# RWKV-7 time mixing: whole 128-row triangular inverses formed ahead of the chains, in place of four multiplications inside each chain

## The chip, the cores and the metric

The kernel runs on one core of a Trainium2 chip. The metric is the device time of one execution in microseconds; the median of three runs stands for the kernel. The core has five engines with queues of their own: TensorE (PE in the profile, its weight loads PEld), VectorE (DVE), ScalarE (ACT), GpSimd (POOL) and SyncE (SP). Each engine takes its instructions in the order of its queue. Matrix products are written to PSUM, a small memory of eight banks, and copied out by ACT or DVE.

## The reference

One decoder layer on 256 tokens of width 2048, all in float32: a SwiGLU feed-forward block, a mixer, a cross-attention into 256 memory rows, a second SwiGLU block, and a final norm. The mixer adds a sliding-window attention and an RWKV-7 time mixing (16 heads of size 64), both gated. What matters here is the recurrence of the time mixing:

```python
def step(S, inp):
    r_t, w_t, k_t, v_t, a_t, b_t = inp
    sa = jnp.einsum('bhij,bhj->bhi', S, a_t)
    S = S * w_t[:, :, None, :] + sa[..., None] * b_t[:, :, None, :] + v_t[..., None] * k_t[:, :, None, :]
    return S, jnp.einsum('bhij,bhj->bhi', S, r_t)
```

Within a block of 128 tokens, the vectors `sa` of all tokens depend on each other through a strictly lower triangular matrix L of 128 x 128 for each head (the products of every `a_t` with every earlier `b_s`, decays included). They solve (I - L) sa = u, where u is known from the values and from the state at the block's start. So each head and block needs the inverse of a triangular 128 x 128 matrix, or its product with u.

## The kernel before, in words

Every large product (feed-forward, projections) splits weights and activations into a high and a low part and multiplies high by high, low by high and high by low: the three lines L407, L408 and L409 in `times`. The weights stream in from memory through SP, ACT casts the high part (L319), DVE subtracts to get the low part (L320), and TensorE takes two of the weight tiles with their three products each at a time. After each six products `product` calls `bg.tick()`.

`Interleave` (`bg`) holds small pieces of other work as Python generators in named groups; a tick lets the first few generators of each group run to their next `yield`, group by group in the order of their declaration. So a `yield` puts about six weight products between two steps, and `idle(n)` puts n ticks there. This sets the order in which the program is written. A planner then orders each engine's queue by its own estimate of the times: what is written first goes first where it is ready, and work that is written later moves ahead where the engine would idle. The buffers are counted per tag (`t4` has 20 of 4 KB a partition); a new tile waits until one is free. The DVE steps of `substitute`, for example, run well before the weight products beside which they are written.

The 1024 features of the time mixing are two halves `h` of eight heads; one `pair(h, j)` treats two heads, e = 0 and 1, and walks through the two blocks c of 128 tokens. Steps that the change touches:

- `removal_keys` (group `ew`) forms L for each half and block and stores it in the DRAM tensor `ld`, rows t, columns s.
- `substitute` loads the 32 x 32 blocks on the diagonal of all 32 matrices, inverts them by 31 steps of forward substitution on DVE (L1125, L1130), and stores them transposed in `xd` (L1132): four blocks i, 32 matrices, u and t.
- `inverse_blocks(h, c)`, called by `pair(h, 0)` for both c, fills two tiles of eight heads on the POOL queue: `x`, the four inverted diagonal blocks (two memsets L1201 and L1202, loads L1205), and `r`, the parts of L to the left of them (loads L1207).
- `pair` masks the products of keys and receptances (`mk`, L1240, from the L177 products, written alternately from rows 0-63 and 64-127 into two banks), forms u (L1249, L1251) and, in the same bank, nt, the product of r and x (L1253): the part of L outside the diagonal blocks, multiplied by the inverted diagonal. It is nilpotent in four steps of 32 rows. So four `stage`s (L1266, each followed by the ACT copy L1271 and a `yield`) give sa: x times u, and then three times nt times the last result plus what was there. The last steps are y (L1290 to L1299) and, for c = 0, the state for the second block (L1283 to L1302).
- `finish` normalizes y for two pairs and multiplies by the gate.

At most three chains (`pair`) run at a time. `substitute`, `receptances` and `values` stand one behind another in the group `ew`; a chain starts when `values(h)` has ended. Beside the chains TensorE does the weight products of r, v and four gates (`L1366`).

Of the kernel before, what the change touches and what calls it, by code (L numbers as in the profile page):

```python
# [7 lines left out]
F32 = mybir.dt.float32  # L8
# [7 lines left out]
P = 128  # L16
# [123 lines left out]
def decoder_layer(ctx: ExitStack, tc: tile.TileContext, a: dict, out: bass.AP):  # L140
    nc = tc.nc
    act, dve, pool, pe = nc.scalar, nc.vector, nc.gpsimd, nc.tensor
# [6 lines left out]
    dram = ctx.enter_context(tc.tile_pool(name="dram", bufs=1, space=DRAM))  # L149
    bg = Interleave()  # L150
    bg.group("const", 1)
    bg.group("feat", 1)
    bg.group("attn", 2)
    bg.group("ew", 1)
    bg.group("chain", 3)
    bg.group("norm", 1)
    bg.group("mem", 1)
# [7 lines left out]
    def mm():  # L165
        return ps.tile([P, 512], F32, tag="mm", name="mm")

    def tr():
        return ps.tile([P, 512], F32, tag="tr", name="tr", bufs=2)
# [9 lines left out]
    def wait_for(name):  # L179
        while name not in bg.seen:  # L180
            yield

    def idle(n):
        for _ in range(n):
            yield
# [38 lines left out]
    for e in range(2):  # L224
        q = slice(64 * e, 64 * e + 64)
# [43 lines left out]
    for entry in weight_plan(a):  # L269
# [4 lines left out]
        w, k0, nk, c0, n = entry  # L274
# [489 lines left out]
    grd = dram.tile([T, D], F32, name="grd")  # L764
    ld = dram.tile([P, 32, P], F32, name="ld")
    xd = dram.tile([4, 32, 32, 32], F32, name="xd")

    def aligned(sp):

# [3 lines left out]
    with tc.tile_pool(name="f1", bufs=1, reuse_waits="tile") as sp:  # L773
        aligned(sp)
        at["pool"] = sp
        x = sp.tile([P, 2, D], F32, name="x")
# [4 lines left out]
        n1 = Norm(g_ffn1)  # L781
# [36 lines left out]
        n2 = hold["n"]  # L818
# [4 lines left out]
    with tc.tile_pool(name="mx", bufs=1, reuse_waits="tile") as sp:  # L823
        aligned(sp)

        def t4(name, shape=(P, 4, T), dt=F32):
            return sp.tile(list(shape), dt, tag="t4", name=name, bufs=N4)
# [285 lines left out]
        def substitute():  # L1113
            yield from idle(4)
            dl = t4("dl", (P, 32, 32))
            for i in range(4):
                q = slice(32 * i, 32 * i + 32)
                pool.dma_start(dl[q], ld[q, :, q].rearrange("t h s -> h t s"))
            xt = t4("xt", (P, 32, 32))
            pool.memset(xt[:], 0.0)  # L1120
            pool.memset(xt[:].rearrange("p u t -> p (u t)")[:, 0 : 32 * 32 : 33], 1.0)
            yield from idle(14)
            tmp = t4("tmp", (P, 32, 32))
            for t in range(1, 32):
                dve.tensor_tensor(  # L1125
                    tmp[:, :t, :t], xt[:, :t, :t],
                    dl[:, t, :t].unsqueeze(1).to_broadcast([P, t, t]), ALU.mult,
                )
                yield
                dve.tensor_reduce(xt[:, :t, t], tmp[:, :t, :t], AX.X, ALU.add)  # L1130
                yield from idle(1 + t // 20)
            pool.dma_start(xd[:].rearrange("i h u t -> (i h) u t"), xt[:])  # L1132
            yield from idle(2)
            bg.seen.add("inverse")

# [59 lines left out]

        xb = {}

        def inverse_blocks(h, c):
            x, r = t4("xb", (P, 8, P)), t4("rb", (P, 8, P))
            o = slice(h * 16 + c * 8, h * 16 + c * 8 + 8)  # L1200
            pool.memset(x[:], 0.0)  # L1201
            pool.memset(r[:], 0.0)  # L1202
            for i in range(4):
                q = slice(32 * i, 32 * i + 32)
                pool.dma_start(x[q, :, q], xd[i, o].rearrange("h u t -> u h t"))  # L1205
                if i:
                    pool.dma_start(r[q, :, : 32 * i], ld[q, o, : 32 * i])  # L1207
            xb[h, c] = x, r

        def small(name):  # L1210
            return sp.tile([P, P], F32, tag="sm", name=name, bufs=14)

        rows = [slice(64 * e, 64 * e + 64) for e in range(2)]
        ek = dict(skip_group_check=True)
        yq = {}

        def pair(h, j):
            yield from wait_for("inverse")
            yield from wait_for(f"ready{h}")
            if j % 2 == 0:  # L1220
                yq[h, j // 2] = sp.tile([P, 2, T], F32, tag="yq", name="yq", bufs=3)
            y = yq[h, j // 2]
            if j == 0:
                for c in range(2):
                    inverse_blocks(h, c)
            if j < 3:
                yield from idle(3 + j)
            ah, bh, kh, rh = at_[h], bt[h], aa[h], rt[h]
            s0 = None
            for c in range(2):  # L1230
                cs_ = slice(c * P, (c + 1) * P)
                mk = sp.tile([P, 2, 3, P], F32, tag="mk", name="mk", bufs=3)
                b = [tr() for _ in range(2)]
                by_turns(
                    (b[e][:, m * P : (m + 1) * P], x1[r, j, cs_], x2[r, j, cs_])
                    for m, (x1, x2) in enumerate(((kh, ah), (kh, rh), (bh, rh)))
                    for e, r in ((1, rows[1]), (0, rows[0]))
                )
                for e in range(2):
                    dve.tensor_tensor(  # L1240
                        mk[:, e].rearrange("p m t -> p (m t)"), b[e][:, : 3 * P],
                        mask3[:].rearrange("p m t -> p (m t)"), ALU.mult,
                    )
                yield
                vp = vtok[h][:, c, j * P : (j + 1) * P]
                x, rr = xb[h, c]
                b = tr()
                for e, r in enumerate(rows):
                    pe.matmul(b[:, r], mk[:, e, 0, :], vp[:, r], start=e == 0, stop=c == 0, **ek)  # L1249
                if c:  # L1250
                    pe.matmul(b[:, :P], ah[:, j, cs_], s0[:], start=False, stop=True, **ek)  # L1251
                for e in range(2):
                    pe.matmul(  # L1253
                        b[:, (2 + e) * P : (3 + e) * P], rr[:, 4 * e + j, :], x[:, 4 * e + j, :],
                        start=False, stop=True, **ek,
                    )
                u = small("u")
                act.copy(u[:], b[:, :P])
                nt = sp.tile([P, 2, P], F32, tag="nt", name="nt", bufs=3)
                act.copy(nt[:], b[:, 2 * P :].rearrange("p (e t) -> p e t", e=2))  # L1260
                yield
                vb = mm()

                def stage(lhs, rhs, o, first, name):
                    for e, r in enumerate(rows):
                        pe.matmul(  # L1266
                            vb[:, o : o + P][:, r], lhs(e), rhs[:, r],
                            start=first and e == 0, stop=True, **ek,
                        )
                    s = small(name)  # L1270
                    act.copy(s[:], vb[:, o : o + P])  # L1271
                    return s

                v0 = stage(lambda e: x[:, 4 * e + j, :], u, 0, True, "v0")
                yield
                v1 = stage(lambda e: nt[:, e, :], v0, 0, False, "v1")
                yield
                w = stage(lambda e: nt[:, e, :], v1, P, False, "w")
                yield
                sa = stage(lambda e: nt[:, e, :], w, 0, False, "sa")  # L1280
                if c == 0:
                    b = tr()
                    pe.transpose(b[:, :P], bh[:, j, cs_], ident[:])  # L1283
                    pe.transpose(b[:, P : 2 * P], kh[:, j, cs_], ident[:])
                    bk = sp.tile([P, 2, P], F32, tag="bk", name="bk", bufs=3)
                    act.copy(bk[:], b[:, : 2 * P].rearrange("p (x f) -> p x f", x=2))
                yield
                b = tr()
                if c:
                    pe.matmul(b[:, :P], s0[:], rh[:, j, cs_], start=True, stop=False, **ek)  # L1290
                for e, r in enumerate(rows):
                    pe.matmul(b[r, :P], vp[:, r], mk[:, e, 1, :], start=c == 0, stop=False, **ek)
                for e, r in enumerate(rows):
                    pe.matmul(b[r, :P], sa[:, r], mk[:, e, 2, :], start=False, stop=True, **ek)
                if c == 0:
                    bs = b[:, P : 2 * P]
                    pe.matmul(bs, bk[:, 0, :], sa[:], start=True, stop=False, **ek)
                    pe.matmul(bs, bk[:, 1, :], vp, start=False, stop=True, **ek)
                act.copy(y[:, j % 2, cs_], b[:, :P])  # L1299
                if c == 0:  # L1300
                    s0 = small("s0")
                    dve.scalar_tensor_tensor(  # L1302
                        s0[:], bs, dec[h][:, j : j + 1], bdup[:], ALU.mult, ALU.mult
                    )
                yield
            bg.seen.add(f"y{4 * h + j}")
# [161 lines left out]
        for h in (0, 2):  # L1468
            b = tr()
# [120 lines left out]
```

## Time and profile before

| | us |
|---|---|
| median of three runs | 2262.45 (2262.22 to 2262.84) |
| the profiled execution | 2258.33 |
| its span | 2256.6 |
| TensorE busy in it | 2240.6 |
| the chains: first L1266 record to last | 1092.5 to 1263.4 |
| store of the 32-row inverses (L1132) | 1008.7 |

The profiled execution lies 4.1 us under the median, so a sum is made against 2258.33 and then moved by that much. A group's line gives the source line, engine, operation, tiles as output<-inputs, shape, count, busy time, the mean duration of one in ns, and the idle time before them with what ended it. For TensorE the shape begins with rows*columns of the array that the record uses, and one float32 product stands as two records, each with its weight load. Records overlap in time; the chain of work (start, duration, what) gives each piece only the time by which it came later than the piece before.

### The profile page before, as it was taken

To read this page: it belongs to the slowest core of one execution; us is meant where nothing else is said; L and a number is where in the kernel's file an instruction comes from. 1 tells how busy PE (TensorE), PEld (TensorE's weight loads), DVE (VectorE), ACT (ScalarE), POOL (GpSimd) and SP (SyncE) were. 2 spreads that over 40 slices of the span, in tenths; PEclk is the share of its full clock that TensorE was granted. 3 is DMA by queue.
4 is the path that set the end of the run, shared out by engine and by line. 5 is a ranking of instruction groups with operands and counts; after the bars stand their busy time and mean duration, and the time that the engine had idled before them with its cause. 6 is when DMAs were issued, how large, how long until landed. Compare 5 with 4: busy or idle time off the path is not lost.

```text
span 2256.6 us, 28302 instructions
## 1 busy us (share of the span) xinstructions
PE 2240.6 (99%) x10588; PEld 1836.1 (81%) x10588; DVE 1740.8 (77%) x2120; ACT 1213.3 (54%) x1611; POOL 130.9 (6%) x184
## 2 busy tenths in 40 slices
PE   9999999999999999999999999999999999999998
PEld 7888888888888777888888888888888888888886
DVE  7988988888987577795444566547898888898887
ACT  6555555555555576444344446556555455555554
POOL 1000000000000002201220030001000000000002
PEclk9999999999999999999999999999999999999999
DMA  7666665565566445766332576547555665555664
GB/s 246 212 223 196 204 207 188 185 212 199 202 199 198 144 143 163 242 207 196 116 108 88 175 258 240 188 159 268 191 203 187 205 204 187 201 195 201 205 203 152
DMA packets 219434, 434.63 MB, mean 193 GB/s; under 512 B 13744, under 2 KB 15872, under 8 KB 219296
## 3 DMA queue, kind: packets, MB, share of 16 engines
q1 hardware_dynamic: 210768, 406.37, 54.0%
q0 software_dynamic: 7952, 25.65, 3.6%
q8 instruction: 83, 1.36, 0.2%
q10 hardware_dynamic: 576, 0.79, 0.1%
q14 instruction: 55, 0.45, 0.1%
HBM read 419.65 MB, written 13.11 MB: 192 GB/s over the span
## 4 chain that ended last, share of the span: by engine, by line
PE 95%; DVE 3%; issue 1%; ACT 1%; DMA 1%; SPq 0%; POOLq 0%; POOL 0%; ACTq 0%; DVEq 0%
PE acc L407 19%; PE acc L409 19%; PE acc L408 19%; PE mm L408 8%; PE mm L409 8%; PE mm L407 8%; PE tr L604 2%; PE tr L408 2%; PE tr L409 2%; PE tr L407 2%; PE mm L1266 1%; DVE lo L320 1%; PE tr L177 1%; PE mm L177 1%; ACT hi L319 0%
## 5 line engine op out<-in xcount | busy, mean ns | idle before, releaser
L319 ACT CAST hi<-raw 128x1024 fp32r<-128x1024 f32 (+1 forms) x770 | 763.7, 1001 | 790.4 <-PE acc L409 387.8
L320 DVE TENSOR_TENSOR lo<-raw,hi 128x1024 fp32r<-128x1024 f32 (+1 forms) x770 | 890.0, 1166 | 369.8 <-ACT hi L319 368.6
L407 PE MATMUL acc<-hi,xhi 128*128 128x512 f32 (+1 forms) x1196 | 475.5, 398 | 2.1 <-ACT hi L319 1.9
L408 PE MATMUL acc<-lo,xhi 128*128 128x512 f32 (+1 forms) x1196 | 465.5, 389 | 1.0 <-DVE lo L320 0.8
L409 PE MATMUL acc<-hi,xlo 128*128 128x512 f32 (+1 forms) x1196 | 465.8, 389 | 0.0
L407 PEld LDWEIGHTS acc<-hi,xhi 128*128 128x128 f32 x1196 | 224.6, 188 | 51.1 <-issue 4.5
L409 PEld LDWEIGHTS acc<-hi,xlo 128*128 128x128 f32 x1196 | 224.5, 188 | 47.9 <-issue 1.7
L408 PEld LDWEIGHTS acc<-lo,xhi 128*128 128x128 f32 x1196 | 224.9, 188 | 46.2 <-DVE lo L320 2.3
L344 ACT CAST thi<-raw 128x1024 fp32r<-128x1024 f32 x160 | 166.0, 1052 | 68.2 <-DVE raw L339 33.3
L345 DVE TENSOR_TENSOR tlo<-raw,thi 128x1024 fp32r<-128x1024 f32 x160 | 192.8, 1218 | 1.3 <-ACT thi L344 1.3
L408 PE MATMUL acc<-lo,hhi 128*128 128x512 f32 x404 | 158.0, 391 | 0.0
L409 PE MATMUL acc<-hi,hlo 128*128 128x512 f32 x404 | 157.9, 391 | 0.0
L407 PE MATMUL acc<-hi,hhi 128*128 128x512 f32 x404 | 157.3, 392 | 0.0
L407 PE MATMUL mm<-hi,xhi 128*128 128x512 f32 x380 | 149.1, 392 | 0.0
L408 PE MATMUL mm<-lo,xhi 128*128 128x512 f32 x380 | 148.1, 390 | 0.0
L409 PE MATMUL mm<-hi,xlo 128*128 128x512 f32 x380 | 148.1, 390 | 0.0
L339 DVE TENSOR_TENSOR raw<-raw 128x1024 f32<-128x1024 f32 x80 | 97.5, 1219 | 19.1 <-DMA raw<-in_ffn_w_up_dram 18.4
L408 PEld LDWEIGHTS acc<-lo,hhi 128*128 128x128 f32 x404 | 75.8, 188 | 17.4 <-DVE lo L320 2.3
L407 PEld LDWEIGHTS acc<-hi,hhi 128*128 128x128 f32 x404 | 75.9, 188 | 16.0 <-DVE x L562 0.9
L409 PEld LDWEIGHTS acc<-hi,hlo 128*128 128x128 f32 x404 | 75.8, 188 | 15.5
L408 PEld LDWEIGHTS mm<-lo,xhi 128*128 128x128 f32 x380 | 71.4, 188 | 15.3 <-DVE lo L320 0.3
L409 PEld LDWEIGHTS mm<-hi,xlo 128*128 128x128 f32 x380 | 71.3, 188 | 14.7
(374 smaller groups left out, 3403.8 us busy)
## 6 DMA issues: line engine op xcount, KB each, us to landing
raw<-in_ffn_w_gate_dram SPq DMA_DIRECT2D x167, 512.0 KB, 3.6
raw<-in_ffn_w_up_dram SPq DMA_DIRECT2D x160, 512.0 KB, 4.6
raw<-in_ffn_w_down_dram SPq DMA_DIRECT2D x152, 512.0 KB, 4.7
raw<-in_w_in_dram SPq DMA_DIRECT2D x136, 512.0 KB, 3.5
raw<-in_w_out_dram SPq DMA_DIRECT2D x32, 512.0 KB, 4.3
raw<-in_ffn_w_down_dram SPq DMA_DIRECT2D x12, 1024.0 KB, 5.0
raw<-in_ffn_w_up_dram SPq DMA_DIRECT2D x8, 1024.0 KB, 6.5
raw<-in_w_proj_attn_dram SPq DMA_DIRECT2D x16, 512.0 KB, 3.5
```

Of the source, the lines that this page charges most:

```text
L177: prev = pe.matmul(*args, start=True, stop=True)
L319: newest["act"] = act.copy(hi[:, s], raw[:, s])
L320: newest["dve"] = dve.tensor_tensor(lo[:, s], raw[:, s], f32(hi[:, s]), ALU.subtract)
L339: dve.tensor_tensor(ta[:], raw[:, 1:3], raw[:, 0:2], ALU.subtract)
L344: act.copy(hi[:, s], t[:])
L345: dve.tensor_tensor(lo[:, s], t[:], f32(hi[:, s]), ALU.subtract)
L407: pe.matmul(o, xh, hi, start=first, stop=False, **how)
L408: pe.matmul(o, xh, lo, start=False, stop=False, **how)
L409: pe.matmul(o, xl, hi, start=False, stop=last, **how)
L604: pe.transpose(b[:, o : o + P], tok[:, t, col : col + P], ident[:])
L1266: pe.matmul(vb[:, o : o + P][:, r], lhs(e), rhs[:, r], start=first and e == 0, stop=True, **ek,)
```

## The change

`substitute` also stores the 32-row inverses the other way round (rows t, columns u) for the first three diagonal blocks, in a new DRAM tensor `xe`: ACT writes the transposed order into the finished scratch tile `tmp`, POOL stores it.

`inverse_blocks` becomes the generator `invert(h, c)` in a group of its own (one at a time, declared ahead of `chain`). It runs from the end of `substitute`, no longer from the first chain. It loads the diagonal blocks x, the blocks r of L, and the blocks xu from `xe`, waits four ticks, and completes the inverse for eight heads in two doublings. First, from 32 to 64 rows: r times x for the blocks 1 and 3 (16 products of 32 x 32, one bank, copied to n1), then a tick later xu times n1 for the blocks 2 and 0 (16 products) and the same product the other way round (8 products), one bank, copied back into x and xu. Then from 64 to 128 rows: 8 products of 64 x 64 and a copy to n2, a tick, 8 products of 64 x 64 and a copy into x. Each head's x is then the whole inverse of its 128-row triangle.

A chain no longer forms nt (L1253, L1260). It waits for its inverse and does one stage in place of four: sa is x times u. There are four ticks for a block in place of seven. The bank `vb` holds one result. The tag `sm` has 10 buffers instead of 14, `nt` is gone, and `xu`, `n1`, `n2` are new.

```diff
+    bg.group("inverse", 1)
     bg.group("chain", 3)
...
+    xe = dram.tile([3, 32, 32, 32], F32, name="xe")
...
             pool.dma_start(xd[:].rearrange("i h u t -> (i h) u t"), xt[:])
+            act.copy(tmp[:96], xt[:96].rearrange("p u t -> p t u"))
+            pool.dma_start(xe[:].rearrange("i h t u -> (i h) t u"), tmp[:96])
             yield from idle(2)
             bg.seen.add("inverse")
...
-        def inverse_blocks(h, c):
-            x, r = t4("xb", (P, 8, P)), t4("rb", (P, 8, P))
+        def invert(h, c):
+            yield from wait_for("inverse")
+            x, r = t4("xb", (P, 8, P)), t4("rb", (P, 8, 96))
+            xu = sp.tile([P, 8, 64], F32, tag="xu", name="xu", bufs=2)
             o = slice(h * 16 + c * 8, h * 16 + c * 8 + 8)
+            q = [slice(32 * i, 32 * i + 32) for i in range(4)]
             pool.memset(x[:], 0.0)
-            pool.memset(r[:], 0.0)
-            for i in range(4):
-                q = slice(32 * i, 32 * i + 32)
-                pool.dma_start(x[q, :, q], xd[i, o].rearrange("h u t -> u h t"))
+            pool.memset(xu[q[0]], 0.0)
+            for i in (1, 3, 2, 0):
+                pool.dma_start(x[q[i], :, q[i]], xd[i, o].rearrange("h u t -> u h t"))
                 if i:
-                    pool.dma_start(r[q, :, : 32 * i], ld[q, o, : 32 * i])
-            xb[h, c] = x, r
+                    pool.dma_start(r[q[i], :, : 32 * i], ld[q[i], o, : 32 * i])
+            for i, to in ((0, q[0]), (2, q[0]), (1, q[1])):
+                pool.dma_start(xu[q[i], :, to], xe[i, o].rearrange("h t u -> t h u"))
+            yield from idle(4)
+
+            def several(bank, products):
+                for to, lhs, rhs in products:
+                    pe.matmul(bank[to], lhs, rhs, start=True, stop=True)
+
+            def cols(n, w):
+                return slice(n * w, n * w + w)
+
+            def heads(bank, rows, w):
+                return bank[rows, : 8 * w].rearrange("p (n t) -> p n t", n=8)
+
+            b = tr()
+            several(b, (
+                ((q[i - 1], cols(n, 32)), r[q[i], n, q[i - 1]], x[q[i], n, q[i]])
+                for n in range(8) for i in (1, 3)
+            ))
+            n1 = sp.tile([P, 8, 32], F32, tag="n1", name="n1", bufs=2)
+            act.copy(n1[q[0]], heads(b, q[0], 32))
+            act.copy(n1[q[2]], heads(b, q[2], 32))
+            yield
+            b = tr()
+            several(b, (
+                ((q[i], cols(n, 32)), xu[q[i], n, q[0]], n1[q[i], n, :])
+                for n in range(8) for i in (2, 0)
+            ))
+            several(b, (
+                ((q[1], cols(n, 32)), n1[q[0], n, :], xu[q[0], n, q[0]]) for n in range(8)
+            ))
+            act.copy(x[q[2], :, q[3]], heads(b, q[2], 32))
+            act.copy(x[q[0], :, q[1]], heads(b, q[0], 32))
+            dve.tensor_copy(xu[q[1], :, q[0]], heads(b, q[1], 32))
+            yield
+            low, high = slice(0, 64), slice(64, 128)
+            b = tr()
+            several(b, (
+                ((low, cols(n, 64)), r[high, n, low], x[high, n, high]) for n in range(8)
+            ))
+            n2_ = sp.tile([64, 8, 64], F32, tag="n2", name="n2", bufs=1)
+            act.copy(n2_[:], heads(b, low, 64))
+            yield
+            b = tr()
+            several(b, (((low, cols(n, 64)), xu[low, n, :], n2_[:, n, :]) for n in range(8)))
+            act.copy(x[low, :, high], heads(b, low, 64))
+            xb[h, c] = x
+            yield
+            bg.seen.add(f"inverse{h}{c}")
+
+        for h in range(2):
+            for c in range(2):
+                bg.spawn("inverse", invert(h, c))
...
         def pair(h, j):
-            yield from wait_for("inverse")
             yield from wait_for(f"ready{h}")
...
             if j == 0:
-                for c in range(2):
-                    inverse_blocks(h, c)
-            if j < 3:
-                yield from idle(3 + j)
+                yield from wait_for(f"inverse{h}0")
+            elif j < 3:
+                yield from idle(j)
...
-                for e in range(2):
-                    pe.matmul(
-                        b[:, (2 + e) * P : (3 + e) * P], rr[:, 4 * e + j, :], x[:, 4 * e + j, :],
-                        start=False, stop=True, **ek,
-                    )
                 u = small("u")
                 act.copy(u[:], b[:, :P])
-                nt = sp.tile([P, 2, P], F32, tag="nt", name="nt", bufs=3)
-                act.copy(nt[:], b[:, 2 * P :].rearrange("p (e t) -> p e t", e=2))
                 yield
...
-                v0 = stage(lambda e: x[:, 4 * e + j, :], u, 0, True, "v0")
-                yield
-                v1 = stage(lambda e: nt[:, e, :], v0, 0, False, "v1")
-                yield
-                w = stage(lambda e: nt[:, e, :], v1, P, False, "w")
-                yield
-                sa = stage(lambda e: nt[:, e, :], w, 0, False, "sa")
+                yield from wait_for(f"inverse{h}{c}")
+                x, vb = xb[h, c], mm()
+                for e, r in enumerate(rows):
+                    pe.matmul(
+                        vb[:, r], x[:, 4 * e + j, :], u[:, r], start=e == 0, stop=True, **ek
+                    )
+                sa = small("sa")
+                act.copy(sa[:], vb[:, :P])
```

More of the change, by code (lines that the diff above doesn't have):

```diff
@@ L1210, in small @@
+            act.copy(x[low, :, high], heads(b, low, 64))
[5 more added lines that the diff above has]
+                bg.spawn("inverse", invert(h, c))
         def small(name):
-            return sp.tile([P, P], F32, tag="sm", name=name, bufs=14)
+            return sp.tile([P, P], F32, tag="sm", name=name, bufs=10)
         rows = [slice(64 * e, 64 * e + 64) for e in range(2)]
@@ L1245, in pair @@
                 vp = vtok[h][:, c, j * P : (j + 1) * P]
-                x, rr = xb[h, c]
                 b = tr()
@@ L1251, in pair @@
                     pe.matmul(b[:, :P], ah[:, j, cs_], s0[:], start=False, stop=True, **ek)
-                for e in range(2):
-                    pe.matmul(
-                        b[:, (2 + e) * P : (3 + e) * P], rr[:, 4 * e + j, :], x[:, 4 * e + j, :],
-                        start=False, stop=True, **ek,
-                    )
                 u = small("u")
                 act.copy(u[:], b[:, :P])
-                nt = sp.tile([P, 2, P], F32, tag="nt", name="nt", bufs=3)
-                act.copy(nt[:], b[:, 2 * P :].rearrange("p (e t) -> p e t", e=2))
                 yield
[L1262 to L1272, printed above, removed]
-                v0 = stage(lambda e: x[:, 4 * e + j, :], u, 0, True, "v0")
-                yield
-                v1 = stage(lambda e: nt[:, e, :], v0, 0, False, "v1")
-                yield
-                w = stage(lambda e: nt[:, e, :], v1, P, False, "w")
-                yield
-                sa = stage(lambda e: nt[:, e, :], w, 0, False, "sa")
+                yield from wait_for(f"inverse{h}{c}")
[6 more added lines that the diff above has]
+                act.copy(sa[:], vb[:, :P])
                 if c == 0:
```

## The prediction

> **What bounds the kernel now.** I read the page first, then the waits of TensorE in the stage that the change touches, then the chain of work of that stage.
>
> ```profile
> span 2256.6 us, 28302 instructions
> PE 2240.6 (99%) x10588; PEld 1836.1 (81%) x10588; DVE 1740.8 (77%) x2120; ACT 1213.3 (54%) x1611; POOL 130.9 (6%) x184
> PEclk9999999999999999999999999999999999999999
> PE 95%; DVE 3%; issue 1%; ACT 1%; DMA 1%; SPq 0%; POOLq 0%; POOL 0%; ACTq 0%; DVEq 0%
> ```
>
> TensorE is busy 99% of the span at full clock and carries 95% of the chain that ended last. The recurrence runs in 1086 to 1273 us, so I take 1050 to 1290 (240 us) as its stage. These are TensorE's waits there (engine, line, waited for, total, times, longest), and busy times in one stretch (PE, PEld, DVE, ACT, POOL):
>
> ```profile
> PE tr L1249 <- DVE mk L1240: 0.2, 1, 0.2
> 1080.00:1120.00 40.00, 40.00 (x270) 32.13 (x270) 18.62 (x29) 15.56 (x36) 4.63 (x9) 1.00 0.34 103
> ```
>
> One wait of 0.2 us in 240: although a chain waits four times in a row for its own copies, TensorE always has a weight product or another chain's step to run meanwhile. DVE, ACT and POOL are under half busy. So shortening a chain's latency is worth nothing by itself; the change is worth the TensorE time that it takes out, less what it puts in. Busy time counts overlapping instructions twice, so I price by the chain of work, whose pieces do not overlap. Its shares of the 240 us:
>
> ```profile
> by line: PE acc L407 20.0%; PE acc L409 18.9%; PE acc L408 18.3%; PE mm L1266 11.6%; PE tr L177 7.2%; PE tr L1253 3.2%; PE tr L1336 2.9%; PE tr L1249 2.8%; PE tr L1292 2.5%; PE tr L1178 1.5%; PE tr L1294 1.5%; PE tr L1327 1.4%; PE tr L1186
> ```
>
> **Removed from TensorE.** Records of the two lines (two records per fp32 matmul: L1253 issues 16 x 2 matmuls and has 64):
>
> ```profile
> L1266 PE MATMUL mm<-v,nt 128*128 128x64 f32 x128 | 17.6, 267 | 0.0
> L1253 PE MATMUL tr<-xb,rb 128*128 128x128 f32 x64 | 10.2, 282 | 0.0
> L1266 PE MATMUL mm<-u,xb 128*128 128x64 f32 x64 | 9.7, 273 | 0.0
> L1266 PE MATMUL mm<-w,nt 128*128 128x64 f32 x64 | 9.3, 268 | 0.0
> ```
>
> L1253 goes whole: 3.2% of 240 = 7.7 us. Of L1266's 256 records only the 64 of the first stage (u) stay: three quarters of 11.6% of 240 = 20.9 us. A third, small term comes from how the pieces stand:
>
> ```profile
> 1086.39 0.87 PE tr L177 x12
> 1087.26 0.43 PE acc L407
> 1087.68 0.23 PE acc L408
> ...
> 1089.73 0.41 PE tr L177 x2
> 1090.14 0.43 PE acc L407
> ...
> 1092.59 0.59 PE mm L1266 x4
> 1093.18 0.29 PE acc L407
> 1093.46 0.23 PE acc L408
> ...
> 1107.24 0.22 PE tr L1294 x4
> ```
>
> A weight product after a full-width stage costs 0.29 instead of 0.23 us. Some 15 such places go, as an estimate from 48 stages that mostly stand in groups: 0.9 us. Removed together: 29.5 us.
>
> **Added to TensorE.** Each of the four inverses (two half layers, two token blocks) issues, for its 8 heads: 16 products of 32x32, then 16 + 8 of 32x32, then 8 and 8 of 64x64. That is 80 narrow and 32 half-wide records, 320 and 128 in all. No such shape is in the trace; the ladder of shapes that are there:
>
> - full width (128 columns of weights, 64 moving): a stage, L1266, about 27.8 us / 256 = 0.11 us a record.
> - half width (64 columns of weights): L1294 does 4 records in 0.22, 0.055 us each. Half the rows (L177, 64 of 128): 12 records in 0.87, entry included.
>
> Half-wide records: bounds 0.055 (L1294) and 0.11 (L1266; L1294 puts two products side by side in one bank, these stand alone). Width sets the price at L1266, whose moving side is only 64 as here, so I take 0.055: 128 x 0.055 = 7.0 us. Narrow records: bounds 0.014 (quartered once more, since most stand in pairs on separate rows and columns of the array) and 0.055 (no narrower record ever cheaper than the half-wide one); 0.11 is the end if neither helps. I take 0.028, half of the half-wide price, as full to half width halved it: 320 x 0.028 = 9.0 us.
>
> Switching: L177 (half the rows) takes 0.87 for 12 records worth 0.66 at 0.055, and the product after it 0.43 instead of 0.23: 0.21 in and 0.20 out, 0.41 us for each piece that stands by itself. The change adds 16 groups (four per inverse). L177's own groups were cut in two in places (x2 above, with its x10 two microseconds later), so I count 20 pieces: 20 x 0.41 = 8.2 us; bounds 10 (groups next to L177 or L1292 share a switch) and 32 (each cut once), 4.1 and 13.1 us.
>
> One rule speaks against the pairing: the Trainium skill, "TensorEngine Tiling (Array Packing)", section Restrictions and Gotchas, says that different row tiles cannot access one PSUM bank at the same time. The first and most of the second group write one bank from two row tiles, while L177's pairs write two banks, so no run here shows it; by that rule the narrow records go one by one and the sum is that of the first rival below instead of mine.
>
> **The other engines, costed at nothing.** Rows of the same stage (ACT and POOL: total us, mean ns, idle before):
>
> ```profile
> L1260 ACT COPY nt<-tr 128x256 f32<-128x256 f32 x16 | 6.1, 379 | 0.0
> L1271 ACT COPY v<-mm 128x128 f32<-128x128 f32 x32 | 8.2, 267 | 11.8 <-PE mm L1266 11.6
> L838 ACT ACTIVATE tok<-acc,rs 128x512 f32<-128x512 f32 x6 | 4.1, 691 | 5.7 <-PE acc L409 5.7
> L319 ACT CAST hi<-raw 128x1024 fp32r<-128x1024 f32 x48 | 50.3, 1048 | 64.3 <-PE acc L409 57.2 <-issue 5.6 <-ACT yq L1299 0.6
> L1205 POOL DMA_DIRECT2D xb<-xd x16 | 9.4, 589 | 0.0
> L1207 POOL DMA_DIRECT2D rb<-ld x12 | 7.0, 583 | 0.0
> L1201 POOL MEMSET xb<- 128x1024 f32 x4 | 3.9, 965 | 0.0
> ```
>
> ACT loses 16 x 0.38 (nt) and 48 x 0.27 (the stages' copies), 18.9 us; it gains per inverse four copies of 256 columns at 0.38 and two of 512 at 0.69, 11.6 us, and once the transposing copy of the 32-row inverses, at least 1.05 (L319's size), at most perhaps twice that. That copy waits for the last DVE reduction of the substitution, and the weight casts queue behind it; they have 64 us of idle in 240. DVE gains four copies. Covered, all of them, by the idle halves of ACT and DVE; without that cover each would cost its own length.
>
> POOL loses four memsets of 1 us and gains four small ones, the store of the transposed inverses, and 12 loads (40 instead of 28): 13 x 0.59 = 7.7 us on a queue that is 12% busy in the stretch above. The four inverses' loads are moved ahead, past the token-shift subtractions (L959) that share the POOL queue; the chain steps that need those come after. SP's weight loads are untouched.
>
> ```profile
> L1205 POOL DMA_DIRECT2D xb<-xd x16: 582/584/622, 1071.1 to 1167.0; - x16
> L1132 POOL DMA_DIRECT2D xd<-xt x1: 568/568/568, 1008.7 to 1008.7; - x1
> DMA to landing us min/median/max: 1.9/3.4/5.2
> L1253 PE MATMUL tr<-xb,rb x64: 275/275/328, 1089.1 to 1257.6; 128*128 128x128 f32 x64
> ```
>
> The 32-row inverses are stored at 1008.7 and first used at 1089.1, 80 us later; the added store and loads fit into that gap. The new wait (a chain's one stage for its inverse) has nothing behind it on TensorE that the planner must hold back: weight products fill in, as they do now.
>
> **Sum.** 29.5 removed - 7.0 - 9.0 - 8.2 added = 5.3 us saved. The profiled execution took 2258.33 us (span 2256.6 and 1.7 around it) and would take 2253.0; the median of the three runs, 2262.45, lies 4.1 above it, so I forecast 2257.1, say 2257. With both cheap ends: 29.5 - 7.0 - 320 x 0.014 - 4.1 = 13.9 us saved, 2248.5. With narrow records at 0.055 and 32 pieces: 7.0 + 17.6 + 13.1 = 37.7 added, 8.2 us lost, 2270.7.
>
> **Rivals.** (1) *Narrow products are no cheaper than half-wide ones*, because issue or the shared bank sets their pace: 320 x 0.055 = 17.6, so 7.0 + 17.6 + 8.2 = 32.8 added, 3.3 us lost, 2265.7: within 0.2%, which is 4.5 us and about what a measurement of this kernel can tell from no change. For: nothing in the trace runs faster than 0.055 a record. Against: every halving in it did halve. (2) *Slower: TensorE waits for the new loads.* One inverse's loads take about ten issues of 0.59, 1.5 us of memsets and 3.4 to land, 10.8 us, while its first product is written four ticks (each six weight products, 1.4 us) after them: 5.4 us of cover if POOL does not run ahead. A wait of 5.4 us in each of four inverses is 21.6, less the 5.3 saved: 16 us lost, 2279; above 2.5 us per inverse it makes the kernel slower than before by over 0.2%. Against: POOL finished today's loads ahead of their use, and TensorE's list of waits shows no DMA. (3) *Cheaper still*: narrow records at 0.014 and shared switches, 2248.5. (4) *The saving is given back by cutting*: the denser chains (four ticks a block instead of seven) share two transposing banks with the inverses, L177 is cut more often; 13 more cuts at 0.41 cancel the 5.3, 2262.4.
>
> **Chances.** Forecast 0.45, (1) 0.20, (2) 0.10, (3) 0.13, (4) 0.12. The forecast's own range is 2253 to 2260, so a fifth of it lies within 0.2%; (1) and (4) fall there mostly, with 0.05 of them beyond it on the slow side, and (2) is slower: faster 0.36 + 0.13 = 0.49, same 0.36, slower 0.15. The range 2250 to 2267 holds all but the far ends of (2) and (3).
>
> **What the changed profile would show.** L1253 gone and L1266's share of the stage a quarter; new lines with 32*32 and 64*64 shapes, four groups of about 0.9, 1.3, 0.9 and 0.9 us plus switches per inverse; TensorE's waits still near zero; the first product of each inverse without a DMA among its releasers. The forecast is wrong if narrow records cost more than 0.045 us each, if pieces of the inverses are far more than 20, or if TensorE idles ahead of them.

## The result, and the profile after

The changed kernel takes 2253.74 us (median of five runs, 2250.95 to 2255.25) where the kernel before took 2262.84 (five runs, 2262.22 to 2263.84): a ratio of 0.9957 with a 95% interval of 0.9942 to 0.9971: 9.1 us faster, 6.6 to 13.1 by the interval. The profiled execution took 2252.11 us. The forecast was 2257 us, and its range holds the result.

The page of the changed kernel, the lines that answer to those of before; code lines up to the inverses have moved by one to four (L408 to L410 are now the weight products, L178 the half-row products):

```profile
span 2250.4 us, 28657 instructions
PE 2232.4 (99%) x10780; PEld 1820.9 (81%) x10780; DVE 1743.0 (77%) x2124; ACT 1208.5 (54%) x1570; POOL 137.6 (6%) x197
PEclk9999999999999999999999999999999999999999
```

TensorE is as full as before, at full clock; ACT has 4.8 us less, POOL 6.7 us more. The gain has to be looked for in TensorE's own work. Where it lies is seen from the first and last starts of the two products that enclose the recurrence, those whose input is ya (the attention's output) and those whose input is yr (the time mixing's output); before, then after:

```profile
L407 PE MATMUL acc<-hi,yahi x64: 389/389/793, 902.8 to 1016.1; 128*128 128x512 f32 x64
L407 PE MATMUL acc<-hi,yrhi x64: 387/389/482, 1301.3 to 1347.0; 128*128 128x512 f32 x64
```

```profile
L408 PE MATMUL acc<-hi,yahi x64: 389/389/793, 904.2 to 1017.5; 128*128 128x512 f32 x64
L408 PE MATMUL acc<-hi,yrhi x64: 387/389/482, 1292.0 to 1337.8; 128*128 128x512 f32 x64
```

From 902.8 to 1301.3 it was 398.4 us (unrounded starts), from 904.2 to 1292.0 it is 387.8: 10.6 us less. I call this stretch the stage. Its chain of work after the change, as shares of the 240 us from 1050 to 1290:

```profile
by line: PE acc L408 21.3%; PE acc L409 20.5%; PE acc L410 20.4%; PE tr L178 6.9%; PE tr L1223 6.4%; PE tr L1307 3.1%; PE mm L1316 3.0%; PE tr L1376 3.0%; PE tr L1332 2.5%; PE tr L1182 1.6%; PE tr L1334 1.5%; PE tr L1367 1.5%; PE tr L1190 1
```

TensorE's only wait in the stretch from 1040 to 1290 is 0.2 us long:

```profile
PE tr L1307 <- DVE mk L1299: 0.2, 1, 0.2
```

The one stage (L1316) has 3.0% where four had 11.6%, L1253 with its 3.2% is gone, and L1223, all products of the inverses, has 6.4%. By the steps from one record's end to the next, summed over the stage:

| TensorE time in the stage | us |
|---|---|
| three stages (v, nt and w, nt) | -20.45 |
| nt (L1253) | -7.57 |
| products of the inverses (L1223), entries included | +15.46 |
| weight products (steps out of a tiled shape among them) | +1.36 |
| half-row products (L177, now L178) | -0.72 |
| all else | +1.34 |
| sum | -10.58 |

The inverses piece by piece (two of the four; start, duration, line, records), and two of their shapes (busy time, mean ns):

```profile
1073.29 0.17 PE tr L1223 x2
1073.90 0.62 PE tr L1223 x30
1076.52 0.18 PE tr L1223 x4
1077.11 0.97 PE tr L1223 x43
1080.56 1.07 PE tr L1223 x16
1084.07 1.07 PE tr L1223 x16
1102.63 0.62 PE tr L1223 x32
1109.82 1.03 PE tr L1223 x47
1116.71 1.07 PE tr L1223 x16
1121.31 1.07 PE tr L1223 x16
...
L1223 PE MATMUL tr<-n,xu 64*64 64x64 f32 x64 | 4.6, 221 | 0.0
L1223 PE MATMUL tr<-xb,rb 32*32 32x32 f32 x128 | 3.0, 192 | 0.0
```

A group of 32 narrow records takes 0.62 us with its entry, 0.019 us each; a group of 16 half-wide ones 1.07. The 16 groups stand in 18 pieces, as two were cut. Entering such a group costs 0.14 us, less than the 0.21 that I had from L177, and the weight product behind it again 0.20. So a narrow record is about 0.017 us on average (6.90 us for 320, less ten entries), a half-wide one 0.058 (8.57 for 128, less eight).

### The profile page after: what moved, and what is told of

Same layout as the page of the kernel before. It is cut to its first block, busy times and chain, and to the rows that moved or that the text cites. A ratio compares the mean times of both kernels' runs of the same rounds, so it can differ in the third digit from the quotient of the medians.

```text
span 2250.4 us, 28657 instructions
## 1 busy us (share of the span) xinstructions
PE 2232.4 (99%) x10780; PEld 1820.9 (81%) x10780; DVE 1743.0 (77%) x2124; ACT 1208.5 (54%) x1570; POOL 137.6 (6%) x197
## 4 chain that ended last, share of the span: by engine, by line
PE 91%; DVE 4%; DMA 2%; issue 1%; ACT 1%; SPq 0%; POOLq 0%; POOL 0%; ACTq 0%; DVEq 0%
PE acc L408 19%; PE acc L409 19%; PE acc L410 19%; PE mm L409 8%; PE mm L410 8%; PE mm L408 8%; PE tr L605 2%; PE tr L409 2%; PE tr L410 1%; DVE lo L321 1%; PE tr L408 1%; DMA raw<-in_ffn_w_up_dram 1%; ACT hi L320 1%; PE tr L178 1%; PE mm L178 1%
## 5 line engine op out<-in xcount | busy, mean ns | idle before, releaser
L320 ACT CAST hi<-raw 128x1024 fp32r<-128x1024 f32 (+1 forms) x770 | 763.6, 1000 | 786.5 <-PE acc L410 386.4
L408 PE MATMUL acc<-hi,xhi 128*128 128x512 f32 (+1 forms) x1196 | 474.7, 397 | 1.8 <-ACT hi L320 1.6
L410 PE MATMUL acc<-hi,xlo 128*128 128x512 f32 (+1 forms) x1196 | 466.3, 390 | 0.0
L408 PEld LDWEIGHTS acc<-hi,xhi 128*128 128x128 f32 x1196 | 224.5, 188 | 51.9 <-issue 5.1
L410 PEld LDWEIGHTS acc<-hi,xlo 128*128 128x128 f32 x1196 | 224.6, 188 | 47.3 <-issue 1.7
L410 PE MATMUL acc<-hi,hlo 128*128 128x512 f32 x404 | 157.8, 391 | 0.0
L408 PE MATMUL acc<-hi,hhi 128*128 128x512 f32 x404 | 157.3, 392 | 0.0
L408 PE MATMUL mm<-hi,xhi 128*128 128x512 f32 x380 | 149.1, 392 | 0.0
L410 PE MATMUL mm<-hi,xlo 128*128 128x512 f32 x380 | 148.1, 390 | 0.0
L340 DVE TENSOR_TENSOR raw<-raw 128x1024 f32<-128x1024 f32 x80 | 97.6, 1221 | 24.9 <-DMA raw<-in_ffn_w_up_dram 22.7
L408 PEld LDWEIGHTS acc<-hi,hhi 128*128 128x128 f32 x404 | 75.9, 188 | 16.1 <-DVE x L563 0.9
L410 PEld LDWEIGHTS acc<-hi,hlo 128*128 128x128 f32 x404 | 75.9, 188 | 15.4
L410 PEld LDWEIGHTS mm<-hi,xlo 128*128 128x128 f32 x380 | 71.3, 188 | 14.7
```

The costliest lines, as they stand in the source:

```text
L320: newest["act"] = act.copy(hi[:, s], raw[:, s])
L340: dve.tensor_tensor(ta[:], raw[:, 1:3], raw[:, 0:2], ALU.subtract)
L408: pe.matmul(o, xh, hi, start=first, stop=False, **how)
L410: pe.matmul(o, xl, hi, start=False, stop=last, **how)
```

## Experiments

Each kernel was timed beside the kernel before on the same chip; "stage" is the stretch from ya to yr in its own trace. Times are compared with the changed kernel's 2253.0 (run again, below) and 387.8. The kernel before had medians of 2261.2 to 2262.7 beside these runs, so differences of 1 or 2 us are read from the stage.

**The changed kernel again**, no edit.

> The changed kernel itself, once more. Work theory (the change is worth the TensorE time it takes out less what it puts in, and nothing else): the stage from the first product with ya to the first with yr is again about 388 us, 10 to 11 us shorter than before, and what the whole time shows beyond or below that comes from the feed-forward blocks, whose waits for weight loads differ from run to run: ratio 0.995 to 0.997. Rival (the change disturbs the second feed-forward block as well, for instance through the phase of the weight loads): that block is again 2 to 3 us longer than before's 667.8.

2253.01 us (2250.91 to 2254.37), ratio 0.9959 (0.9946 to 0.9971); stage 387.8 once more, both as expected. The stage repeats to a tenth; the second feed-forward block took 670.9 us against 670.3 in the first trace. So the rival keeps its point, and the next run looks at it from the other side.

**The kernel before again**, no edit.

> The kernel before, once more, for its trace. The first profile of it took 2258.3 us where its timed runs take 2261 to 2265, while its stage should be fixed by the order of TensorE's queue. Theory (the difference of a few us between profiles lies in the feed-forward blocks' waits for weight loads, in both kernels alike): the stage from ya to yr is again 398.4 us, and the two feed-forward segments are 2 to 4 us longer in sum than the 767.6 and 667.8 of the first profile. Rival (the changed kernel's longer feed-forward segments are an effect of the change): they are again about 767.6 and 667.8.

2261.22 us; stage 398.4, as expected. The stretch up to the attention was 769.5 us (767.6 in the first profile), and so no different from the changed kernel's 769.0 and 769.6; the second feed-forward block took 667.4. Half of the expectation holds. The waits of DVE for a load of up-weights (summed, count, longest), in two profiles of the kernel before and then in two of the changed kernel:

```profile
DVE raw L339 <- DMA raw<-in_ffn_w_up_dram: 18.4, 15, 2.2
DVE raw L339 <- DMA raw<-in_ffn_w_up_dram: 21.7, 17, 2.3
```

```profile
DVE raw L340 <- DMA raw<-in_ffn_w_up_dram: 22.7, 21, 2.6
DVE raw L340 <- DMA raw<-in_ffn_w_up_dram: 24.3, 20, 2.6
```

These waits move by 3 us between two profiles of one kernel. But the second feed-forward block took 667.8, 667.4 and 668.4 us in the three traces of kernels with the old chains, and 668.2 to 671.7 in the eleven with the new ones (mean 670.0), though its program is the same. That would give back some 2 us of the 10.6, and would fit the 9.1 of the medians; what causes it was not tried. The medians do not need it: their interval, 6.6 to 13.1 us, covers 10.6.

**Every small product twice.**

```diff
-                for to, lhs, rhs in products:
+                for to, lhs, rhs in 2 * list(products):
```

> Every list of small products in the inverses is issued twice in a row into the same bank (the second pass writes the same values). Work theory with the prices read from the changed kernel (narrow records 0.017 us, half-wide 0.0575, switches unchanged): 320 x 0.017 + 128 x 0.0575 = 12.8 us slower than the changed kernel, so about 2 to 3 us slower than before. Narrow-price rival (0.055 a record once they no longer run ahead of the queue): 24.9 us slower than the changed kernel.

2265.19 us, 12.2 over the changed kernel and 3.3 over the kernel before (ratio 1.0014, 1.0005 to 1.0024); stage +14.7. Groups of the first inverses in the chain of work (start, duration, line, records):

```profile
1106.79 1.13 PE tr L1223 x64
1113.79 2.04 PE tr L1223 x95
1121.22 2.00 PE tr L1223 x32
```

Doubling adds 0.51 us to 32 narrow records and 0.93 to 16 half-wide ones; L1223 grows by 13.4 us. The prices hold when nothing but the work is doubled, and the rival's 24.9 us is out.

**The three stages back, as dummies.**

```diff
                 act.copy(sa[:], vb[:, :P])
+                v = sa
+                for k in range(3):
+                    yield
+                    o = slice((1 + k) * P, (2 + k) * P)
+                    for r in rows:
+                        pe.matmul(
+                            vb[:, o][:, r], x[:, 4 + j, :], v[:, r], start=False, stop=True, **ek
+                        )
+                    v = small("v")
+                    act.copy(v[:], vb[:, o])
```

> The three dropped stages come back into every chain as dependent dummies (products with another head's inverse, each copied out, a tick apart; no result is used), while the forming of nt stays away. Work theory: three quarters of the old stage time, 20.5 us, comes back, no more and no less, so about 11 us slower than before. Latency theory (part of the gain is that a chain has fewer dependent steps): clearly more than 20.5 us over the changed kernel.

2273.09 us, 20.1 over the changed kernel; stage +21.1.

```profile
by line: PE acc L408 19.3%; PE acc L409 18.3%; PE acc L410 17.6%; PE mm L1326 8.5%; PE tr L178 6.6%; PE tr L1223 6.2%; PE tr L1307 2.9%; PE tr L1386 2.8%; PE mm L1316 2.7%; PE tr L1342 2.4%; PE tr L1344 1.5%; PE tr L1182 1.5%; PE tr L1377 1
```

The dummies (L1326) have 8.5% of 250 us, 21.3 us, and that is the whole loss. The chain's three extra dependent steps cost their TensorE time and nothing for being dependent.

**Seven ticks a block, without the work.**

```diff
+                yield from idle(3)
                 yield from wait_for(f"inverse{h}{c}")
```

> Three empty ticks before each chain's one stage, so a block takes seven ticks as before the change; no work added. Work theory: within 2 us of the changed kernel. Latency theory: a good part of the gain goes, at least 4 us slower than the changed kernel. Cutting theory (denser chains cut the groups of half-row products and pay switches for it): 1 to 4 us faster than the changed kernel, with fewer than 24 pieces of half-row products.

2255.52 us (2250.53 to 2255.96). The median lies 2.5 us over the changed kernel's, where at most 2 was expected, but the range covers that kernel's; the stage is 388.1 against 387.8, with 25 pieces of half-row products against 24, so the rest lies outside it. Neither the chain's latency nor its density matters here. That also takes away the fourth rival's ground: the groups are not cut more because the chains are denser (before the change there were 26 pieces).

**One row tile after the other.**

```diff
-                for n in range(8) for i in (1, 3)
+                for i in (1, 3) for n in range(8)
...
-                for n in range(8) for i in (2, 0)
+                for i in (2, 0) for n in range(8)
```

> The narrow products of the first and second group are issued block by block (all eight heads of one 32-row tile, then all eight of the other) instead of alternating. Pairing theory: the narrow records rise from 0.02 us to about 0.03 each in those two groups (256 records): 2 to 3 us more in the inverse lines. Rival (a narrow record costs the same in any order, the pairs share one bank anyway): no difference.

One run: 2254.30 us, stage 390.8, 3.0 more.

```profile
1073.64 1.17 PE tr L1223 x32
1077.84 1.18 PE tr L1223 x40
1081.50 1.07 PE tr L1223 x16
1103.57 1.02 PE tr L1223 x32
```

The same 32 records take 1.02 to 1.17 us instead of 0.62; all 320 go from 6.90 to 10.07. Less entries that is 0.0275 us a record, the 0.028 of the prediction: that was nearly the price of a narrow record alone. From one record's end to the next, a record behind another of its own tile takes 0.031 to 0.032 us, and a pair from two row tiles 0.032 in the changed kernel (steps of 0.025 and 0.007). So two that alternate between row tiles run side by side, in different partitions of one bank.

**Two banks for the two row tiles.**

```diff
             b = tr()
+            d = mm()
...
-                for n in range(8) for i in (1, 3)
+            for n in range(8):
+                for bank, i in ((b, 1), (d, 3)):
```

> The two row tiles of the first and of the second group of an inverse write to two banks (one of tag tr, one of tag mm) instead of one. Theory (alternating row tiles already run side by side in one bank): the narrow lines take 6.9 us again, within 0.5. By the rule weighed in the prediction (row tiles cannot use one bank at the same time): they fall, by up to half, 2 to 3 us.

(The second group likewise.) One run: 2251.30 us, stage 389.3; the narrow records take 8.38 us, not 6.90 and not less, so neither expectation holds for the sum. Part of the records were issued one tile at a time, most of them in the second groups of two inverses, and those take 0.03 us each; that the two banks came free at different times would explain it, but was not tried. The bank can be seen where the tiles did alternate: the first groups of the last three inverses, from 1102.8, 1137.7 and 1163.4, take 0.62 us for 32 records with two banks, as they do with one. So sharing a bank does not keep the tiles apart.

**No idle ticks ahead of an inverse.**

```diff
-            yield from idle(4)
```

> The four empty ticks between an inverse's loads and its first product are taken away. Theory (POOL runs far ahead and the planner fills in other work): TensorE's waits stay near zero and the stage stays within 2 us of 387.8. Rival (the four ticks are what hides the loads): TensorE waits for the loads, 2 to 5 us in each of four inverses.

One run: 2254.68 us, stage 389.5; TensorE's products wait for nothing in the stage, and the first inverse product starts at 1071.4 instead of 1073.2. So the rival falls, but POOL does not fetch far ahead either. It issues the loads of r and x for the first inverse at 1068.6 to 1072.1, and they land at 1071.0 to 1075.5. The first group is cut in two around them:

```profile
1071.47 0.17 PE tr L1221 x2
1075.06 0.62 PE tr L1221 x30
```

In the 3.4 us between stand weight products. It is this other work in TensorE's order that covers the loads; the stage became 1.7 us longer.

**Both blocks of a half inverted side by side.** `invert(h)` runs each of the four steps for c = 0 and c = 1 in turn, from a bank of tr and one of mm, and shares the ticks.

```diff
-        def invert(h, c):
+        def invert(h):
...
-            b = tr()
+            b = banks()
+            for c in two:
```

(`banks` gives one bank of each tag; every `several` and every copy is repeated for both c, with two buffers of n2.)

> Both token blocks of a half layer are inverted side by side: each of the four groups is issued for 16 heads, from two banks, so there are 8 places instead of 16 where the narrow and half-wide groups begin. Work theory with a switch of about 0.35 us in and out: 8 fewer, 2.8 us faster than the changed kernel. Waiting rival: the first product of a half now needs twice as many loads, 20 issues of 0.59 us, and TensorE waits 5 us or more for them.

2253.35 us (2251.60 to 2261.29; three of twelve runs took 2259 or more), ratio 0.9965 (0.9955 to 0.9974): no gain; stage 388.9. The half-wide groups do stand together, in 5 pieces instead of 8, but the narrow ones are cut into 12 instead of 10 and the half-row products into 27 instead of 24. No wait of TensorE appears. What was saved in one place came back in another.

**The masks' products in mm banks.**

```diff
-                b = [tr() for _ in range(2)]
+                b = [mm() for _ in range(2)]
                 by_turns(
```

> The half-row products of each chain (masked keys and receptances) write to two banks of the tag mm, which the stages hardly use now, instead of both banks of tr. Cutting theory (those groups are cut because the second tr bank is not free): 16 groups stand in about 16 pieces instead of 24, 8 x 0.45 = 3.6 us faster than the changed kernel. Rival (they are cut for other reasons): no difference.

2246.53 us (2244.05 to 2249.39), ratio 0.9927 (0.9915 to 0.9939): 6.5 us under the changed kernel, where 3.6 was expected; stage 381.6, 6.3 less. Some of the groups in the changed kernel, and then with the edit:

```profile
1185.46 0.41 PE tr L178 x2
1187.01 0.86 PE tr L178 x10
1200.93 0.42 PE tr L178 x2
1202.24 0.86 PE tr L178 x10
1215.95 0.41 PE tr L178 x2
1217.03 0.86 PE tr L178 x10
```

```profile
1184.90 0.87 PE mm L178 x12
1188.37 0.87 PE mm L178 x12
1199.31 0.87 PE mm L178 x12
1213.52 0.87 PE mm L178 x12
```

One matmul (two records) went ahead into the first bank, and the rest, which begins with the second bank, came a microsecond or more later in these lines; now nearly every group stands whole, 18 pieces instead of 24. The lines themselves lose 3.0 us and the weight products of the stage 3.1: a group falls back into a weight product 11 times instead of 22, since several now stand directly ahead of another tiled group.

**Both.**

> Both of the last two changes together. If they are independent: 2.8 + 3.6 = 6.4 us faster than the changed kernel. If they compete for the mm banks: less than the better of the two.

2245.72 us, ratio 0.9925 (0.9914 to 0.9937), stage 380.9: within 1 us of the masks' edit alone, as the joined inverses bring nothing. The 6.4 expected is met, but not by the sum of two gains. Both versions beat the two kernels of this document.

**The masks' edit in the kernel before** (the same diff).

> The kernel before with the half-row products of the chains written to two banks of tag mm instead of both banks of tr. If the cutting of those groups is a matter of the tr banks alone and not of the change: they stand in fewer than 26 pieces here too, and the kernel gains 3 to 6 us. If the four stages, which hold an mm bank for a whole block, now block them: no gain, or a loss.

2256.44 us, ratio 0.9978 (0.9968 to 0.9987), 4.7 us faster than before; 20 pieces instead of 26, stage 393.1. The cutting is older than the change and nearly independent of it: the two gains in the stage are 10.6 and 5.3 apart, 15.9 in sum, and 16.8 together (398.4 to 381.6).

## Why the prediction was right

*What bounds.* TensorE's work alone. The runs with dummies, empty ticks and doubled products each moved the time by about the TensorE time they added (20.1 for 21.3, 12.2 for 13.4, and with empty ticks 2.5, within the spread, for 0.3).

*Removed, 29.5.* 28.0: 7.57 and 20.45 for the 7.7 and 20.9 read from the shares. The third term was 0.9 us for 15 weight products at 0.29 behind full-width products. By the steps, 31 stood there before (behind L1266 and L1249) and 13 stand there now (behind L1316 and L1307): 18 fewer, 1.0 us. Weight products together still got 1.36 dearer, for the steps out of the new shapes.

*Half-wide records, 0.055 each.* 0.058.

*Narrow records, 0.028 each, 9.0 us.* 0.017, 5.5 us less entries. This is the term that was mis-sized most, by 3.5 us. The ladder of shapes gave the price of about one product at a time; that the alternating ones would also share the time in pairs I had only as the cheap end, 0.014. The rule that spoke against pairing, that different row tiles cannot access one PSUM bank at the same time, in the Trainium skill, "TensorEngine Tiling (Array Packing)", section Restrictions and Gotchas, does not agree with the trace, as far as the tiles write to different partitions of the bank: 0.62 us for 32 alternating records, in one bank or in two, against 1.02 to 1.17 one tile after the other. The measurement decides. The prediction also priced that case wrongly: it equated records one by one with rival (1), 0.055 each, while one tile after the other measured 0.0275, which is the forecast's own price.

*Switches, 20 pieces at 0.41, 8.2 us.* 18 pieces, 0.14 in and, for the 11 that a weight product follows, 0.20 out; with the other exits that is an estimated 5 to 6 us: the count was nearly right and the entry too dear, being that of half-row products (0.25 by their first records).

*Sum.* 5.3 saved was forecast, 10.6 measured in the stage, 9.1 in the medians; the forecast's own range, 2253 to 2260, just holds 2253.74. With the measured terms (28.0 and 1.0 removed) the same sum gives 29.0 - 7.4 - 5.5 - about 5.5 = 10.6. So the mechanism and the direction were right, and the saving was forecast at about half its size, because narrow records and entries were both priced too high; that 2257 lies close to the result says little, since the whole change is 0.4% of the time. Whether anything outside the stage gives part of the gain back is open (the second feed-forward block, above).

*Other engines at nothing.* ACT's transposing copy and POOL's extra work, in the changed kernel:

```profile
L1135 ACT COPY tmp<-xt x1: 2138/2138/2138, 1009.6 to 1009.6; 96x1024 f32<-96x1024 f32 x1
POOL xu L1218 <- DMA xe<-tmp: 6.1, 1, 6.1
POOL xu L1212 <- PE tr L1223: 5.1, 1, 5.1
```

The copy took 2.14 us, just over the upper bound of twice 1.05; POOL waited 6.1 us for the stored transposed blocks and 5.1 for a buffer, and neither reached TensorE, whose one wait in the stage is the 0.2 us above.

*Rivals.* (1) fell with the doubled products (13.4 us for what would have been 24.9), (2) with the run without idle ticks, (4) with the run of seven ticks. (3) was closer on the narrow records, 0.014 where 0.017 was measured, and wrong about shared switches: 18 pieces stand where it had 10.

## What to carry to other kernels

Where one engine has no idle time, price a change in that engine's time alone, from the steps of the chain of work, and check whether dependent steps cost anything by adding them back as dummies. Small products on TensorE were cheap here where they alternated between row tiles; entering and leaving the tiled shapes cost as much as some 20 narrow records. So look for groups that are cut in two for want of a second bank: the cut of an older group was worth 6.5 us here, two thirds of the whole change, for two letters.

## What had not been expected

A weight product behind any of the small shapes took the same 0.20 us more (0.43 against 0.23), but entering differed, by the first records behind a weight product: 0.25 for 64 rows, 0.20 for 64 columns (L1332), about 0.14 for 32x32 and 64x64. A strided copy that turns 32 x 32 blocks took twice the time of a plain one with as many elements in each partition (L1135 against L320, 2.14 against 1.05 us). And a second bank for the paired products made them slower in sum, 8.38 against 6.90 us, since part of them no longer alternated.
